# A streaming encoder layer: norm squares and block differences on VectorE, sample tokens at once, w_out summands a unit ahead, early sums first

## The chip, the core and the metric

The kernel runs on one core of a Trainium2 chip. The metric is the device time of one execution in microseconds; the time before is the median of three. In the rows PE is TensorE (PEld its weight loads), DVE is VectorE, ACT is ScalarE, POOL is GpSimd, and SP issues DMAs; ACTq and SPq are the DMA issues of ScalarE and SyncE.

## The reference

One layer is computed for 1024 prompt tokens and 32 sample tokens of width 1024:

```python
x = x + 0.5 * swiglu(rms_norm(x, ffn1_norm), ffn1_w_in, ffn1_w_out)   # hidden width 2816
h = rms_norm(x, mix_norm)
sq, sk, sv, hq, hf, hi, hg = split(h @ w_in)                          # 7 x 512 columns
sb_o = rms_norm(stick_breaking(rms_norm(sq), rms_norm(sk), sv))       # 8 heads of 64
o_h = rms_norm(hgrn2_scan(...)) * silu(hg)                            # 4 heads, 128 x 128
x = x + concat(sb_o, o_h) @ w_out
x = x + 0.5 * swiglu(rms_norm(x, ffn2_norm), ffn2_w_in, ffn2_w_out)
```

All is fp32. Besides the two x it returns the new keys, values and states.

## The kernel before

Everything is held transposed: 128 partitions are features, columns are tokens. A matrix product is three passes of fp32r matmuls, since each operand is split into a high part (a ScalarE copy, line 157) and a low part (a VectorE subtraction, line 158); `split` does both. The w_in product of each FFN, with its 2 x 2 blocks, and the second product are made of seven block products in place of eight, as in Strassen's scheme, so sums and differences of blocks are needed on both sides.

The stages follow one another: FFN1 (0 to about 735 us of the span), the mixers (to about 1440), the rest of w_out and FFN2. The order of instructions on each engine is written out when the program is built, from a planner's estimate of when each is ready and, among those ready, by the order of the source; inside `high_priority()` an instruction goes ahead of all others that are ready. On the chip each engine and each DMA queue then runs its list in order.

`prep_first` and `prep_rest` (from line 327) make the operands of an FFN's first product out of the four token-and-feature blocks b11, b12, b21, b22, once for each of two column parts of 256 and 272 columns. `prep_rest` takes four differences (line 336, the helper `sub`), each 1024 or 1088 columns wide; three run on VectorE and one, b22 - b12, on GpSimd. Line 316 scales a block by its norm.

`early_products` (line 343) runs the first two of the seven products for a few weight columns j (6 in FFN1, 8 in FFN2) before the operands of the others are there. ScalarE copies a product out of PSUM into a tile `e` (line 363), or VectorE adds one (line 365), and ScalarE's queue stores `e` to `pd` (line 367). In FFN2 from j = 2 the second product is accumulated in the same PSUM bank after the first was copied out. The tiles `e` are three buffers under the tag `xp`, which the mixers' small tiles and the w_out summands also use. `split_a` splits the weights of j + 2 (`wh`, `wl`), in two halves in FFN2 and whole in FFN1. The sums of the other weights (`rS`, lines 430 to 433) run on GpSimd for j = 0.

`Second.run` (from line 674) does an FFN's second product in 77 steps of 24 matmuls; line 643/644 split the weights (1024 columns), 654/655 the tokens `th`, `tl` (528 columns), 690 adds up blocks of x. In FFN1, `on1` calls `mix_in` in the last 22 steps and after each of the last four chunks, 16 times in all, for one chunk of 128 features and one half of the tokens. `mix_in` (line 1490) works on 512 prompt and then 16 sample columns: high part (1498), low part (1499), square (1501, 1504) and the sum of squares into `g.r` (1505, on GpSimd). `mix_factor` (1508) makes the norm's factor from `g.r`; that of half of the prompt tokens and of the sample tokens runs late, amid the mixers' first projections.

`mix_stream` (from line 1417) is the larger part of w_out: 8 chunks of 128 outputs in 3 token groups, 24 units of 18 matmuls. `g.slabs.get` loads weights (line 173, on SP). Each unit loads its summand `xp` from `xd` (line 1434, on SP), adds it to the product (1444, VectorE) and stores the sum (1445, on SP). `mix_units` (line 1459) follows with the rest of w_out.

Of the kernel before, what the change touches and what calls it, by code (L numbers as in the profile page):

```python
# [8 lines left out]
F32 = mybir.dt.float32  # L9
F32R = mybir.dt.float32r  # L10
U8 = mybir.dt.uint8
AF = mybir.ActivationFunctionType
ALU = mybir.AluOpType
AX = mybir.AxisListType
# [3 lines left out]
P = 128  # L18
D = 1024
KC = D // P  # L20
TP = 1024
TS = 32
T = TP + TS
GROUPS = ((0, 384), (384, 768), (768, T))
NG = len(GROUPS)
TG = 384
# [6 lines left out]
PASSES = ((0, 0), (0, 1), (1, 0))  # L33
# [113 lines left out]
def gs(n):  # L147
    return slice(*GROUPS[n])


def gw(n):
    return GROUPS[n][1] - GROUPS[n][0]


def split(nc, hi, lo, src):

    nc.scalar.activation(hi, src, AF.Copy)  # L157
    return nc.vector.tensor_tensor(out=lo, in0=src, in1=hi, op=ALU.subtract)  # L158
# [96 lines left out]
BW = 528  # L255
NB = 2
HK = KC // 2
# [70 lines left out]
def prep_rest(g, xc, rr, gain, xs, dst):  # L328

    nc = g.nc  # L330
    if xc is not None:
        for k in range(KC):
            scaled(nc.vector, dst[:, k, 1], xc[:, k, 1], gain, rr[:, 1], k)
    b11, b12 = dst[:, 0:HK, 0, :], dst[:, 0:HK, 1, :]
    b21, b22 = dst[:, HK:KC, 0, :], dst[:, HK:KC, 1, :]
    sub = lambda eng, out, p, q: eng.tensor_tensor(out=out, in0=p, in1=q, op=ALU.subtract)
    sub(nc.vector, b11, b12, b11)
    sub(nc.gpsimd, b12, b22, b12)
    split(nc, *xs["B22"], b22)
    sub(nc.vector, b22, b22, b11)  # L340
    sub(nc.vector, b21, b21, b22)
    for o, src in (("T2", b22), ("T1", b11), ("T3", b12), ("T4", b21)):
        split(nc, *xs[o], src)


def early_products(g, psp, xs, wts, pd, early, shared, between=None):

    nc = g.nc
    steps = [(p, j, c) for c in range(2) for j in range(2) for p in (1, 2)]
    for j in range(2, early):  # L350
        steps += [(1, j, 0), (1, j, 1), (2, j, 0), (2, j, 1)] if shared else [(p, j, c) for c in range(2) for p in (1, 2)]
    banks, tmps, done = {}, {}, 0
    for p, j, c in steps:
        w, cc = CW[c], cols(c)
        add = p == 2 and shared and j > 1
        wn, xn = PRODUCTS[p]
        if not add:
            banks[j, c] = psp.tile([P, 512], F32, name="bk", tag="bk", bufs=8)
        ps = banks[j, c][:, 0:w]
        products(g, ps, wts.get(j, wn), xs[c][xn], not add)  # L360
        tmp = g.wp.tile([P, CW[1]], F32, name=f"e{p}", tag="xp", bufs=3)[:, 0:w]
        if p == 1 or add:
            nc.scalar.activation(tmp, ps, AF.Copy)  # L363
        else:
            nc.vector.tensor_tensor(out=tmp, in0=ps, in1=tmps[j, c], op=ALU.add)
        tmps[j, c] = tmp
        nc.scalar.dma_start(pd[:, j, p - 1, cc], tmp)
        if p == 2:
            if c == 1 and j + 2 < early:
                wts.split_a(j + 2, 2 if shared else 1)  # L370
                if j + 4 < early:
                    wts.load_a(j + 4)
            if between is not None:
                between(done)
            done += 1
# [1043 lines left out]
def mix_stream(g, m, psp, xs, mix, xd):  # L1419

    nc = g.nc
    while not m.dup_done[3]:
        yield None
    for i, c in enumerate(MIX_FIRST):
        raw = m.sp.tile([P, T], F32, name="mraw", tag=("qn", "kn")[i % 2], bufs=1)
        nc.sync.dma_start(raw, mix[c])
        split(nc, xs(0, c), xs(1, c), raw)
    yield 5.0
    for d in range(KC):
        wt = g.slabs.get()  # L1430
        for n in range(NG):
            w = gw(n)
            xp = g.wp.tile([P, TG], F32, name="xp", tag="xp", bufs=3)
            nc.sync.dma_start(xp[:, 0:w], xd[:, d, gs(n)])
            ps = psp.tile([P, 512], F32, name="ps", tag="pp", bufs=2)
            for k, c in enumerate(MIX_FIRST):
                for i, (a, b) in enumerate(PASSES):
                    nc.tensor.matmul(ps[:, 0:w], wt[a][:, k, :], xs(b, c)[:, gs(n)],  # L1438
                                     start=(k == 0 and i == 0), stop=(k == 5 and i == len(PASSES) - 1))
                if n and k == 3:  # L1440
                    g.slabs.split_next()
                if k % 2:
                    yield 1.0
            nc.vector.tensor_tensor(out=xp[:, 0:w], in0=ps[:, 0:w], in1=xp[:, 0:w], op=ALU.add)
            nc.sync.dma_start(xd[:, d, gs(n)], xp[:, 0:w])
        m.spilled.append(d)
        m.fetch()

# [42 lines left out]
def mix_in(g, xs, pool, x, d, b):  # L1491

    nc = g.nc
    gain = g.gm[:, d:d + 1]
    for at, w, to in ((0, 512, 512 * b), (512, 16, TP + 16 * b)):
        src = x[:, d, b, at:at + w]
        hi, lo, acc = (t[:, to:to + w] for t in (xs(0, d), xs(1, d), g.r))
        nc.scalar.activation(hi, src, AF.Copy, scale=gain)
        nc.vector.scalar_tensor_tensor(out=lo, in0=src, scalar=gain, in1=hi, op0=ALU.mult, op1=ALU.subtract)
        if d == 0:  # L1500
            nc.scalar.activation(acc, src, AF.Square)
        else:
            sq = pool.tile([P, w], F32, name=f"nsq{w}", tag=f"nsq{w}", bufs=2)
            nc.scalar.activation(sq, src, AF.Square)  # L1504
            nc.gpsimd.tensor_tensor(out=acc, in0=acc, in1=sq, op=ALU.add)  # L1505


def mix_factor(g, ms, a, e):
# [14 lines left out]
def tile_layer(ctx: ExitStack, tc: tile.TileContext, *aps):  # L1523
# [132 lines left out]
    def on1(p, k):  # L1656
        if (p, k) == (6, FH - 1):
            qs.close()
            mx.stack, mx.pool = pool_of("xnp")
            mx.a = mx.pool.tile([P, 2, len(MIX_FIRST), T], F32R, name="xs_a", tag="xs_a", bufs=1)  # L1660
            mx.b = mx.pool.tile([P, 2, len(MIX_LAST), T], F32R, name="xs_b", tag="xs_b", bufs=1)
            tables(g, EXP_LN)
            todo.extend([(d, ROLE[0]) for d in range(HK)] + [(d, ROLE[1]) for d in range(HK)])
        elif (p, k) == (7, FH - 1):
            todo.extend((d, ROLE[1]) for d in range(HK, KC))
        elif p == "d":
            if k == 0:
                mix_factor(g, psp.tile([P, 512], F32, name="bk", tag="bk", bufs=8), 512 * ROLE[1], 512 * ROLE[1] + 512)
            mix_in(g, xs_mix, fbp, sec.x, HK + k, ROLE[0])
        elif todo and (p == 7 or p == 4 and k > 1):  # L1670
            with behind(g, sec.hi, sec.lo):
                mix_in(g, xs_mix, fbp, sec.x, *todo.pop(0))
        if (p, k) in ((4, FH - 3), ("d", 0)):
            g.slabs.ahead(1 if p == 4 else 2, whole=False)
        if (p, k) in ((4, FH - 2), ("d", 1)):
            for _ in range(2):
                g.slabs.split_next()
# [191 lines left out]
```

## Time and profile before

| | |
|---|---|
| median of 3 executions | 2187.49 us (2186.66 to 2188.24) |
| the profiled execution | 2183.27 us |
| its span, first to last instruction | 2181.5 us |
| granted TensorE clock, mean over the span | 0.995 of full speed |

The profile is of one execution, which took 4.22 us less than the median; 1.77 us of it lie outside its span. All stretches below are in microseconds from the span's start. A row of a timeline gives start, duration, engine, line, operation, the tile written and those read, the shapes, and in brackets the engine's idle time before it with what ended it. A waits row gives the waiter, what it waited for, microseconds in total, times, and the longest.

### The profile page before, as it was taken

Reading aid. Unit: us, or ns where it says so; the run is one execution under the profiler, and the core shown is the slowest. Engines: PE = TensorE matmul, PEld = TensorE weight load, DVE = VectorE, ACT = ScalarE, POOL = GpSimd, SP = SyncE. Lnnn points to the kernel's source line nnn. Section 1 sums busy time; section 2 is a strip of 40 time slices with the busy share of each in tenths; the row PEclk is TensorE's granted clock in tenths of the full one; section 3 lists DMA queues with packets and bytes.
Section 4 is the critical chain, followed back from the end, with each engine's and each line's share of the span. In section 5 each row is a group of like instructions: output and inputs, shape, how many; then the busy total and the mean of one; then the engine's idle time right before and its main releaser. Section 6 shows DMA issues by size and latency. Waiting matters only on the chain.

```text
span 2181.5 us, 41553 instructions
## 1 busy us (share of the span) xinstructions
PE 2123.6 (97%) x16331; PEld 2073.3 (95%) x16331; DVE 1476.6 (68%) x2537; ACT 937.5 (43%) x1836; POOL 631.9 (29%) x905
## 2 busy tenths in 40 slices
PE   8999999999999999999999999999999999999998
PEld 8999999999999899989899898889999999999998
DVE  5877666664678658778678688548677665655675
ACT  6423333333446555555564564235323332334443
POOL 1455544441002410311311311122555354420000
PEclk9999999999999999999999999999999999999999
DMA  8565454547534311120111212564775455466343
GB/s 242 177 215 171 149 175 147 160 145 262 211 117 158 104 55 29 44 70 21 54 59 29 69 58 88 169 199 139 224 225 179 160 163 163 155 212 241 123 149 124
DMA packets 328804, 307.28 MB, mean 141 GB/s; under 512 B 26592, under 2 KB 284896, under 8 KB 328608
## 3 DMA queue, kind: packets, MB, share of 16 engines
q1 hardware_dynamic: 259456, 264.75, 37.2%
q10 hardware_dynamic: 68672, 38.25, 6.0%
q8 instruction: 128, 2.10, 0.4%
q0 software_dynamic: 480, 1.62, 0.2%
q14 instruction: 68, 0.56, 0.1%
HBM read 208.46 MB, written 96.11 MB: 140 GB/s over the span
## 4 chain that ended last, share of the span: by engine, by line
PE 54%; DVE 4%; DMA 3%; POOL 2%; ACT 1%; issue 1%; SPq 0%; ACTq 0%; DVEq 0%; POOLq 0%
PE bk L382 17%; PE pp L833 14%; PE bk L697 10%; PE pl L1339 2%; PE av L1109 1%; PE ps L1438 1%; PE pt L1090 1%; DMA xd<-xp 1%; PE ps L1459 1%; PE z L1145 1%; PE z L1144 1%; DVE t L1003 1%; DMA oraw<-in_ffn_w_out_dram 1%; DMA xp<-xd 1%; PE pb L242 1%
## 5 line engine op out<-in xcount | busy, mean ns | idle before, releaser
L697 PE MATMUL bk<-tl,wh 128*128 128x256 f32 x1232 | 351.2, 285 | 4.6 <-DVE tl L655 4.5
L697 PE MATMUL bk<-th,wl 128*128 128x256 f32 x1232 | 350.0, 284 | 0.0
L697 PE MATMUL bk<-th,wh 128*128 128x256 f32 x1232 | 349.2, 285 | 0.5 <-ACT th L654 0.5
L833 PE MATMUL pp<-xs_a,wh 128*128 128x384 f32 (+1 forms) x1008 | 258.2, 338 | 0.0
L697 PEld LDWEIGHTS bk<-tl,wh 128*128 128x128 f32 x1232 | 232.5, 189 | 6.0 <-DVE tl L655 6.0
L697 PEld LDWEIGHTS bk<-th,wh 128*128 128x128 f32 x1232 | 231.7, 189 | 1.2 <-ACT th L654 0.9
L697 PEld LDWEIGHTS bk<-th,wl 128*128 128x128 f32 x1232 | 232.5, 189 | 0.2 <-issue 0.2
L833 PEld LDWEIGHTS pp<-xs_a,wh 128*128 128x128 f32 x1008 | 168.7, 189 | 5.9 <-issue 4.1
L644 DVE SCALAR_TENSOR_TENSOR wl<-oraw,wh 128x1024 fp32r<-128x1024 f32 x84 | 98.0, 1167 | 106.4 <-ACT wh L643 106.4
L537 POOL TENSOR_TENSOR gt<-gt,b 128x256 f32<-128x256 f32 x88 | 72.7, 826 | 325.1 <-ACT gt L536 325.1
L833 PE MATMUL pp<-xs_a,wl 128*128 128x384 f32 (+1 forms) x504 | 163.9, 325 | 0.0
L643 ACT ACTIVATE wh<-oraw 128x1024 fp32r<-128x1024 f32 x84 | 83.7, 996 | 147.4 <-PE bk L697 127.8
L382 PE MATMUL bk<-ops_a,wh 128*128 128x272 f32 (+1 forms) x704 | 132.9, 289 | 2.4 <-ACT e L363 2.4
L536 ACT ACTIVATE gt<-gt 128x256 f32<-128x256 f32 x88 | 37.3, 423 | 218.8 <-DVE gt L503 218.8
L157 ACT ACTIVATE wh<-wraw 128x512 fp32r<-128x512 f32 (+2 forms) x122 | 89.0, 749 | 93.4 <-PE pp L833 26.2
L158 DVE TENSOR_TENSOR wl<-wraw,wh 128x512 fp32r<-128x512 f32 (+2 forms) x122 | 107.7, 896 | 31.5 <-ACT wh L157 30.8
L382 PEld LDWEIGHTS bk<-ops_a,wh 128*128 128x128 f32 x704 | 111.2, 192 | 3.0 <-ACT e L363 2.9
L541 POOL TENSOR_TENSOR gt<-gt,b 128x256 f32<-128x256 f32 x88 | 90.1, 1024 | 78.2 <-DVE b L503 78.2
L382 PE MATMUL bk<-ops_a,wl 128*128 128x272 f32 (+1 forms) x352 | 101.1, 288 | 2.6 <-DVE wl L158 2.6
L503 DVE TENSOR_TENSOR gt<-bk,p 128x256 f32<-128x256 f32 (+1 forms) x60 | 25.9, 432 | 109.7 <-PE bk L382 107.8
L833 PEld LDWEIGHTS pp<-xs_a,wl 128*128 128x128 f32 x504 | 94.7, 188 | 0.1
L1505 POOL TENSOR_TENSOR rstd<-rstd,nsq 128x512 f32<-128x512 f32 (+1 forms) x28 | 33.4, 1218 | 205.1 <-ACT nsq L1504 205.1
(464 smaller groups left out, 6930.9 us busy)
## 6 DMA issues: line engine op xcount, KB each, us to landing
wraw<-in_ffn_w_in_dram SPq DMA_DIRECT2D x58, 512.0 KB, 4.3
oraw<-in_ffn_w_out_dram SPq DMA_DIRECT2D x94, 256.0 KB, 4.5
sd<-osum SPq DMA_DIRECT2D x44, 512.0 KB, 3.1
gd<-gt SPq DMA_DIRECT2D x42, 528.0 KB, 4.9
braw<-in_ffn_w_in_dram ACTq DMA_DIRECT2D x42, 512.0 KB, 4.3
oraw<-sd SPq DMA_DIRECT2D x40, 512.0 KB, 3.6
oraw<-in_ffn_w_out_dram SPq DMA_DIRECT2D x30, 512.0 KB, 3.3
wraw<-in_w_in_dram SPq DMA_DIRECT2D x28, 512.0 KB, 3.6
```

The lines of the kernel that those rows point to most:

```text
L157: nc.scalar.activation(hi, src, AF.Copy)
L158: return nc.vector.tensor_tensor(out=lo, in0=src, in1=hi, op=ALU.subtract)
L382: mm = g.nc.tensor.matmul(ps, wt[x][:, kk, :], xt[y][:, kk, :], start=(first and kk == 0 and n == 0), stop=(kk == HK - 1 and n == len(PASS ...
L536: silu = nc.scalar.activation(gt[:, 1, cc], gt[:, 1, cc], AF.Silu)
L537: nc.gpsimd.tensor_tensor(out=gt[:, 1, cc], in0=gt[:, 1, cc], in1=s["b2"], op=ALU.mult)
L541: last = nc.gpsimd.tensor_tensor(out=gt[:, 0, cc], in0=gt[:, 0, cc], in1=s["b1"], op=ALU.mult)
L643: nc.scalar.activation(h, r, AF.Copy, scale=0.5)
L644: nc.vector.scalar_tensor_tensor(out=l, in0=r, scalar=0.5, in1=h, op0=ALU.mult, op1=ALU.subtract)
L697: nc.tensor.matmul(ps, wt[a][:, d * P:(d + 1) * P], xt[b][:, cols(c)], start=(k == 0 and n == 0), stop=(k == FH - 1 and n == len(PASSES) - 1))
L833: g.filler = nc.tensor.matmul(ps[:, 0:gw(n)], wt[a][:, k, :], xs(b, k)[:, gs(n)], start=(k == 0 and j == 0), stop=(k == KC - 1 and j == le ...
L1339: nc.tensor.matmul(pl[0:L, c, 0:hl].rearrange("p (b m) -> p b m", m=m_), k[:, cs(b, c)], qr, start=True, stop=True)
L1505: nc.gpsimd.tensor_tensor(out=acc, in0=acc, in1=sq, op=ALU.add)
```

## The change

Five edits:

- The fourth difference of `prep_rest`, b22 - b12, moves from GpSimd to VectorE, for both column parts of both FFNs.
- In `early_products` the copies and adds out of PSUM get high priority, and so do the splits of the weights of j + 2, which are now in two halves in FFN1 too.
- In `mix_stream` the load of a unit's summand is issued a unit ahead, that of the first unit before the loop.
- `mix_in` leaves out the sample columns, and its sum of squares moves from GpSimd to VectorE.
- A new function, `mix_in_sample`, does the sample columns of all eight chunks at once, after the last `mix_in` of the second product: one square, one reduction, one multiplication by the gain, and three splits.

```diff
-    sub(nc.gpsimd, b12, b22, b12)
+    sub(nc.vector, b12, b22, b12)
...
-            if p == 1 or add:
-                nc.scalar.activation(tmp, ps, AF.Copy)
-            else:
-                nc.vector.tensor_tensor(out=tmp, in0=ps, in1=tmps[j, c], op=ALU.add)
+        with g.tc.high_priority():
+            if p == 1 or add:
+                nc.scalar.activation(tmp, ps, AF.Copy)
+            else:
+                nc.vector.tensor_tensor(out=tmp, in0=ps, in1=tmps[j, c], op=ALU.add)
...
-                wts.split_a(j + 2, 2 if shared else 1)
+                with g.tc.high_priority():
+                    wts.split_a(j + 2, 2)
...
+    units = [(d, n) for d in range(KC) for n in range(NG)]
+    def summand(d, n):
+        xp = g.wp.tile([P, TG], F32, name="xp", tag="xp", bufs=3)
+        nc.sync.dma_start(xp[:, 0:gw(n)], xd[:, d, gs(n)])
+        return xp
+    nxt = summand(*units[0])
...
+    for u, (d, n) in enumerate(units):
+        if n == 0:
+            wt = g.slabs.get()
+        w, xp = gw(n), nxt
+        if u + 1 < len(units):
+            nxt = summand(*units[u + 1])
...
-    for at, w, to in ((0, 512, 512 * b), (512, 16, TP + 16 * b)):
...
-            nc.gpsimd.tensor_tensor(out=acc, in0=acc, in1=sq, op=ALU.add)
+        nc.vector.tensor_tensor(out=acc, in0=acc, in1=sq, op=ALU.add)
+def mix_in_sample(g, mx, pool, x):
+    src = x[:, :, :, 512:BW]
+    t = pool.tile([P, KC, NB, 16], F32, name="smx", tag="nsq", bufs=2)
+    nc.scalar.activation(t, src, AF.Square)
+    nc.vector.tensor_reduce(out=g.r[:, TP:T].rearrange("p (b s) -> p b s", b=NB),
+                            in_=t.rearrange("p k b s -> p b s k"), axis=AX.X, op=ALU.add)
+    t = pool.tile([P, KC, NB * 16], F32, name="smx", tag="nsq", bufs=2)
+    nc.vector.tensor_tensor(out=t.rearrange("p k (b s) -> p k b s", b=NB), in0=src,
+                            in1=g.gm[:, :, None, None].broadcast_to([P, KC, NB, 16]), op=ALU.mult)
+    for dst, ks in ((mx.a[:, :, 0:3, TP:T], slice(0, 3)), (mx.b[:, :, :, TP:T], slice(3, 8, 4)),
+                    (mx.a[:, :, 3:6, TP:T], slice(4, 7))):
+        split(nc, dst[:, 0], dst[:, 1], t[:, ks])
...
             mix_in(g, xs_mix, fbp, sec.x, HK + k, ROLE[0])
+            if k == HK - 1:
+                mix_in_sample(g, mx, fbp, sec.x)
```

## Rows read from the trace of the kernel before

**Rows 1.** The page's part 1: busy us, share of the span, instructions.
```profile
PE 2123.6 (97%) x16331; PEld 2073.3 (95%) x16331; DVE 1476.6 (68%) x2537; ACT 937.5 (43%) x1836; POOL 631.9 (29%) x905
```

**Rows 2.** Waits of TensorE, whole span: total us, times, longest us.
```profile
PE bk L697 <- DVE tl L655: 4.5, 4, 2.5
...
PE bk L382 <- DVE wl L158: 3.5, 2, 2.6
...
PE bk L382 <- ACT e L363: 2.4, 2, 1.7
PE ps L1459 <- DVE xp L1444: 2.1, 1, 2.1
...
PE bk L382 <- ACT S2h L157: 1.4, 1, 1.4
...
PE ps L1438 <- DVE xp L1444: 0.9, 1, 0.9
```

**Rows 3.** Windows: stretch, length, busy (count) PE PEld DVE ACT POOL, clock, DMA.
```profile
682.16:685.57 3.41, 3.19 (x14) 3.19 (x15) 3.41 (x6) 1.06 (x4) 1.93 (x2) 0.50 0.72 232
1494.53:1497.94 3.41, 3.41 (x18) 3.41 (x17) 3.41 (x6) 1.94 (x4) 0.00 (x0) 0.50 0.79 240
560.00:563.41 3.41, 3.41 (x30) 3.41 (x29) 1.31 (x2) 1.17 (x2) 0.00 (x0) 1.00 0.83 321
```

**Rows 4.** Timeline of VectorE, 1486 to 1494 us, FFN2's early products.
```profile
1485.57 0.48 DVE L316 SCALAR_TENSOR_TENSOR x<-x,g,rr 128x256 f32<-128x256 f32 x1
...
1488.57 2.64 DVE L316 SCALAR_TENSOR_TENSOR x<-x,g,rr 128x272 f32<-128x272 f32 x1
...
1491.48 1.21 DVE L336 TENSOR_TENSOR x<-x 128x1024 f32<-128x1024 f32 x1
1492.61 1.28 DVE L158 TENSOR_TENSOR wl<-wraw,wh 128x512 fp32r<-128x512 f32 x2
```

**Rows 5.** Timeline of GpSimd in the same stretch: the difference that moves.
```profile
1487.59 3.31 POOL L336 TENSOR_TENSOR x<-x 128x1024 f32<-128x1024 f32 x1 [11.95 <-DVE x L336]
```

**Rows 6.** Timeline of VectorE, 669 to 684 us, mix_in amid FFN1's second product.
```profile
670.17 0.89 DVE L1499 SCALAR_TENSOR_TENSOR xs_a<-x,gm,xs_a 128x512 fp32r<-128x512 f32 x2
...
673.28 0.70 DVE L655 TENSOR_TENSOR tl<-rw,th 128x528 fp32r<-128x528 f32 x1
673.90 1.94 DVE L1499 SCALAR_TENSOR_TENSOR xs_a<-x,gm,xs_a 128x512 fp32r<-128x512 f32 x2
...
679.39 2.30 DVE L644 SCALAR_TENSOR_TENSOR wl<-oraw,wh 128x1024 fp32r<-128x1024 f32 x1
```

**Rows 7.** Timeline of GpSimd, 660 to 750 us: the sums that move.
```profile
673.21 8.56 POOL L1505 TENSOR_TENSOR rstd<-rstd,nsq 128x512 f32<-128x512 f32 x6 [166.49 <-ACT nsq L1504]
```

**Rows 8.** Windows, columns as in rows 3: from the first mix_in steps to TensorE's wait.
```profile
664.90:682.38 17.48, 14.42 (x114) 13.78 (x112) 17.48 (x19) 17.45 (x40) 8.56 (x6) 0.99 0.56 187
```

**Rows 9.** Timeline of VectorE, 745 to 748 us: the last mix_in.
```profile
745.60 0.91 DVE L1499 SCALAR_TENSOR_TENSOR xs_b<-x,gm,xs_b 128x512 fp32r<-128x512 f32 x2
```

**Rows 10.** Timeline of TensorE, 754 to 757 us: first reader of the sample columns' sums.
```profile
754.01 1.17 PE L1510 MATMUL nms<-rstd,ones 128*128 128x512 f32 x4
```

**Rows 11.** Timeline of ScalarE, 1524 to 1531 us, end of FFN2's early products.
```profile
1528.61 1.10 ACT L157 ACTIVATE T41h<-x 128x1088 fp32r<-128x1088 f32 x1
...
1529.61 0.37 ACT L363 ACTIVATE e<-bk 128x256 f32<-128x256 f32 x1
```

**Rows 12.** Timeline of SP's queue, 1398 to 1412 us, w_out.
```profile
1404.93 0.33 SPq L1445 DMA_DIRECT2D xd<-xp  x1
1405.55 0.33 SPq L1434 DMA_DIRECT2D xp<-xd  x1
```

**Rows 13.** The summand loads, line 1434: count, first and last start, time to landing.
```profile
L1434 SPq DMA_DIRECT2D xp<-xd x24: 319/324/530, 1323.4 to 1439.2; - x24
...
DMA to landing us min/median/max: 2.1/2.8/5.8
```

**Rows 14.** The stores of the sums, line 1445: time to landing.
```profile
DMA to landing us min/median/max: 1.7/2.6/6.0
```

More of the change, by code (lines that the diff above doesn't have):

```diff
@@ L1427, in mix_stream @@
         split(nc, xs(0, c), xs(1, c), raw)
-    yield 5.0
[L1429 to L1445, printed above, removed]
+    units = [(d, n) for d in range(KC) for n in range(NG)]
[4 more added lines that the diff above has]
+    nxt = summand(*units[0])
+    yield 5.0
+    for u, (d, n) in enumerate(units):
[4 more added lines that the diff above has]
+            nxt = summand(*units[u + 1])
+        ps = psp.tile([P, 512], F32, name="ps", tag="pp", bufs=2)
+        for k, c in enumerate(MIX_FIRST):
+            for i, (a, b) in enumerate(PASSES):
+                nc.tensor.matmul(ps[:, 0:w], wt[a][:, k, :], xs(b, c)[:, gs(n)],
+                                 start=(k == 0 and i == 0), stop=(k == 5 and i == len(PASSES) - 1))
+            if n and k == 3:
+                g.slabs.split_next()
+            if k % 2:
+                yield 1.0
+        nc.vector.tensor_tensor(out=xp[:, 0:w], in0=ps[:, 0:w], in1=xp[:, 0:w], op=ALU.add)
+        nc.sync.dma_start(xd[:, d, gs(n)], xp[:, 0:w])
+        if n < NG - 1:
+            continue
         m.spilled.append(d)
@@ L1494, in mix_in @@
     gain = g.gm[:, d:d + 1]
-    for at, w, to in ((0, 512, 512 * b), (512, 16, TP + 16 * b)):
[L1496 to L1504, printed above, removed]
-            nc.gpsimd.tensor_tensor(out=acc, in0=acc, in1=sq, op=ALU.add)
+    at = slice(512 * b, 512 * b + 512)
+    src = x[:, d, b, 0:512]
+    hi, lo, acc = (t[:, at] for t in (xs(0, d), xs(1, d), g.r))
+    nc.scalar.activation(hi, src, AF.Copy, scale=gain)
+    nc.vector.scalar_tensor_tensor(out=lo, in0=src, scalar=gain, in1=hi, op0=ALU.mult, op1=ALU.subtract)
+    if d == 0:
+        nc.scalar.activation(acc, src, AF.Square)
+    else:
+        sq = pool.tile([P, 512], F32, name="nsq", tag="nsq", bufs=2)
+        nc.scalar.activation(sq, src, AF.Square)
+        nc.vector.tensor_tensor(out=acc, in0=acc, in1=sq, op=ALU.add)
+def mix_in_sample(g, mx, pool, x):
+    nc = g.nc
+    src = x[:, :, :, 512:BW]
[9 more added lines that the diff above has]
+        split(nc, dst[:, 0], dst[:, 1], t[:, ks])
 def mix_factor(g, ms, a, e):
```

## Prediction

> **What bounds the kernel now.** The page first: TensorE is busy for 2123.6 of 2181.5 us [rows 1]. The change adds and removes no matmul, so at most those 57.9 idle us are to be had, and what a lowered clock costs. So TensorE's waits come next. Of the groups that the five edits can touch, the reader sees six: on the low part of the second product's tokens `tl` 4.5 us (longest 2.5), on the early weights `wl` 3.5 (2.6), on the early tiles `e` 2.4, on the w_out sums `xp` 2.1 and 0.9, and on the first weight sums S2 1.4 [rows 2]. Then the windows: two stretches of 3.41 us around the two longest of these were granted 0.50 of the clock, which is its 1.2 GHz level, against 1.00 (2.4 GHz) elsewhere. They hold 14 and 18 matmuls, where 3.41 us at the full level hold 30 [rows 3]. TensorE had just stood still for 2.5 and 2.6 us. One matmul takes 3.41/30 = 0.114 us, so the drop costs 12 x 0.114 = 1.4 us in the second stretch; in the first, with 3.19 us of busy time, 28 would have fitted, so 14 x 0.114 = 1.6. I count 1.5 for a drop. Last, VectorE and GpSimd at the two longest waits, part by part below.
>
> **The difference b22 - b12.** On GpSimd it ran from 1487.59 to 1490.90 us [rows 5]. On VectorE a scaling of 272 columns began at 1488.57 and took 2.64 us, ending 0.3 us behind GpSimd; its sibling of 256 columns took 0.48 [rows 4]. So 2.16 us of VectorE were lost while GpSimd ran. Behind the stretched instruction stood the next `e` sum, the difference at 1491.48 (1.21) and then the two halves of `wl` at 1492.61 [rows 4], for which TensorE waited 2.6 us [rows 2]. After the change VectorE makes the difference itself, at 1.21 as its like of 1024 columns. The loss of 2.16 goes, and the 1.21 comes in. If the halves of `wl`, now of high priority, go ahead of both differences, they are 2.16 + 1.21 = 3.4 us early and the wait of 2.6 is gone, with its clock drop. If they stay behind both, they are 2.16 - 1.21 = 0.95 early. I take the first, 2.6 + 1.5 = 4.1 us; ends 0.95 and 4.1. The other three differences stand where rows 2 shows no wait of this size; VectorE's idle time covers them (32% of the span, [rows 1]), and without that cover they cost up to 3 x 1.21 = 3.6.
>
> **The sums of squares.** From 664.90 to 682.38 us VectorE was busy without a gap, and ScalarE for 17.45 of 17.48 [rows 8]; at the end TensorE waits 2.5 for `tl`. A pair of low parts took 0.89 us when GpSimd stood still and 1.94 with its sums alongside [rows 6, 7]; one more such pair lies in the stretch. The weights' low part at 679.39 took 2.30, where 1024 columns alone take about 1.21 [rows 4, 6]. On VectorE a sum over 512 columns should take what 528 do, 0.70 [rows 6]. So in this stretch: the first pair loses its 16 columns (0.89 to 0.70, a gain of 0.19), two pairs become 0.70 + 0.70 in place of 1.94 (0.54 each), and the weights' split gets 1.09 back: 0.19 + 1.08 + 1.09 = 2.36. ScalarE loses two short instructions per call, so it isn't late in VectorE's place. The wait shrinks from 2.5 to about 0.15, the smaller waits on `tl` there go with it, and the clock drop ends: 2.36 + 1.5 = 3.9. Ends: with both waits there (2.9) gone 4.4; if VectorE won nothing back from GpSimd, three sums of 0.70 on a full engine would lose 2.1.
>
> The Trainium skill speaks against this part: its Perfetto Trace Analysis, section Optimizing Scalar/DVE Operations, says that where VectorE is saturated, moving work to ScalarE or even GpSimd may make sense, and adds that the two share a read port, so it may not help. By the first half the sum would hold the loss of 2.1 where I count a gain of 3.9, and the time would be 6.0 us more. The stretched rows here agree with its second half.
>
> **The sample columns at once.** Per call two instructions on ScalarE, one on VectorE and one on GpSimd go, 16 times; nine come, once, four on ScalarE and five on VectorE, none with more than 256 columns, so at most 0.48 each [rows 4]: 2.4 us on VectorE. They come after the last low parts, which end at 746.5 [rows 9], and so end by about 749; the first reader of their sums starts at 754.01 [rows 10]. That cover of 5 us makes them free. They stand on VectorE ahead of the first projections' reductions, which without a gap would cost up to 1.
>
> **Weights in halves.** In FFN1 the other wait on `wl` is 3.5 - 2.6 = 0.9 us [rows 2]. TensorE needs the first half first, and that is ready one half's time, 0.64 [rows 4], earlier on VectorE and about as much on ScalarE, so the wait goes. But what is late next is S2 (1.4 us, [rows 2]), whose sums wait for stored tiles to come back and not for TensorE: arriving 0.9 sooner, it waits 0.9 longer. I take 0; ends 0.9 lost and 0.9 won.
>
> **Early sums first.** At the end of FFN2's early products ScalarE made an operand for 1.10 us at 1528.61 and the copy `e` after it, at 1529.61 [rows 11]; TensorE waited for that copy. With priority it goes ahead of the operand: 1.0 us. The waits for `e` come to 2.4 [rows 2]; the rest stands behind weight sums of GpSimd, which this edit doesn't move. Ends 0 and 2.4; I take 1.0.
>
> **The summands.** A load at 1405.55 stood on SP behind a store at 1404.93 that needed VectorE's sum [rows 12]. A unit earlier in the source, it goes ahead of that store, and ahead of the next weights' two loads where a new chunk begins; the add that TensorE waited 0.9 for then has its summand. The later wait, 2.1 with a drop, I leave in the sum: only three buffers carry loads and stores, and a load can't start before an older store has landed, however early it is asked for. Ends 0 and 0.9 + 2.1 + 1.5 = 4.5; I take 0.9.
>
> **The sum.** 4.1 + 3.9 + 0 + 0 + 1.0 + 0.9 = 9.9 us. The profiled execution took 2183.27, so 2173.4; it lies 4.2 below the median of 2187.49, which by the same sum goes to 2177.6 (ratio 0.9955).
>
> **Rivals.** About 0.2%, 4.4 us, is what a measurement of this kernel can tell from no change, so the borders of no change are 2183.1 and 2191.9.
>
> Everything goes (4.1, 4.4, 0.9, 2.4, 4.5, together 16.3): 2171.2. For it speak the many short waits with one cause; against, that orders are planned anew and some waits come back.
>
> The waits come back: the halves of `wl` stay behind both differences (0.95, clock drop kept) and the moved sums stand ahead of `tl` (two of 0.70 off 2.36 leave 0.95); nothing else: 1.9 won, 2185.6, no change. For it speaks that VectorE is full in both places [rows 4, 8].
>
> The moved sums only load VectorE: nothing comes back from GpSimd, and three sums of 0.70 on a full engine lose 2.1 where 3.9 were counted, so 9.9 - 6.0 = 3.9 are won, 2183.6. For it speaks the full engine [rows 8], against it the stretched pairs [rows 6]. It is what the first half of the sentence of the Trainium skill's Perfetto Trace Analysis, Optimizing Scalar/DVE Operations, comes to here.
>
> Slower, by the summands' buffers. From 1323.4 to 1439.2 the 24 loads start 115.8/23 = 5.0 us apart [rows 13], so each of three buffers may be held for 15.0. It is held for the load (median 2.8), VectorE's sum (0.5) and the store (2.6, [rows 14]), 5.9; asked for a unit ahead, for 5.0 more: 10.9, and nothing is lost. With the longest landings, 5.8 and 6.0, it is 17.3, so 5.8 a unit, 0.8 x 24 = 19 us lost, against 9.0 from the other edits: 2197.5. It decides from 15.0 on, where load and store together take 9.5 us rather than 5.4.
>
> **How the numbers follow.** Chances: forecast 0.53, everything goes 0.13, waits come back 0.18, moved sums only load VectorE 0.06, slower 0.10. The forecast's own range, with its terms' ends, is 2173 to 2182. The range 2169 to 2188 takes in all but the slower rival and some 0.05 beyond its ends. Faster 0.66, the first two; same 0.24, the next two; slower 0.10.
>
> **What would show it.** Right: no difference on GpSimd, and no VectorE scaling over 0.6 us in the early products; low parts of 512 columns at 0.70 throughout; TensorE's waits on `wl` near 0 and on `tl` under 2.5 in all; two clock drops fewer. Wrong: the granted clock still 0.50 in FFN1's last steps or FFN2's early products, a longer wait on S2, ScalarE held up for an `xp` buffer, or new waits in the mixers, whose order is planned anew.

## The result, and the profile after

The changed kernel takes 2173.66 us, the kernel before beside it 2186.64 (medians of 8 executions each): ratio 0.9946, 95% interval 0.9933 to 0.9959. Measured again later it was 0.9958 (0.9945 to 0.9972). The forecast, 2177.6 from 2187.49, is a ratio of 0.9955. The profiled execution's span is 2172.3 us, after 2181.5. In the changed kernel line numbers are one or two higher in FFN1's and FFN2's code (L382 is L384) and ten to twelve higher in w_out and `mix_in`.

The page's part 1, as in [rows 1]; GpSimd lost 46 us of work and VectorE, which took it over, 7:

```profile
PE 2118.7 (98%) x16331; PEld 2069.1 (95%) x16331; DVE 1469.8 (68%) x2548; ACT 933.2 (43%) x1812; POOL 585.6 (27%) x873
```

TensorE's waits, as in [rows 2]:

```profile
PE bk L384 <- DVE S4l L158: 7.3, 5, 2.9
PE bk L752 <- issue: 3.4, 1, 3.4
...
PE ps L1448 <- ACT wh L157: 2.0, 1, 2.0
PE ms L1499 <- POOL rr L1481: 1.6, 1, 1.6
PE ps L1471 <- DVE xp L1454: 1.5, 1, 1.5
...
PE bk L384 <- ACT e L364: 1.1, 2, 0.8
...
PE bk L699 <- DVE tl L657: 0.8, 2, 0.6
```

Two groups of the kernel before that [rows 2] leaves out:

```profile
PE bk L382 <- DVE S4l L158: 4.1, 5, 1.5
...
PE bk L750 <- issue: 1.9, 1, 1.9
```

The reader sees what went: the early products' wait on `wl`, 3.5 us, is gone from the list, `tl` is down from 4.5 to 0.8, `e` from 2.4 to 1.1. And what came: in FFN1 the wait for the last rows' transposes (L752, "issue") was 1.9 and is 3.4. The waits on the weight sums S4 were 4.1 over the whole span and are 7.3: 2.8 and 4.3 of it in FFN1, 1.3 and 2.9 in FFN2. In w_out there is a wait on `wh`, in its end one on `rr`. The windows, as in [rows 3]: the two drops shown of before are gone, and two stand in FFN1, behind the two longer waits (besides the one at the end there are five in the whole trace before, two here). The third row stands behind a wait of 2.5 us in w_out's rest; here the clock stays up.

```profile
46.87:50.28 3.41, 3.41 (x19) 3.41 (x18) 1.95 (x3) 2.42 (x3) 1.27 (x1) 0.50 1.18 292
101.48:104.89 3.41, 3.41 (x16) 3.41 (x16) 3.14 (x7) 0.00 (x0) 1.66 (x2) 0.50 0.88 288
1464.65:1468.06 3.41, 2.44 (x18) 2.23 (x18) 3.30 (x8) 2.70 (x8) 2.25 (x3) 1.00 0.41 141
```

VectorE's timeline in FFN2's early products, which answers to [rows 4]: five scalings take 2.06 together where one of 272 columns took 2.64, the difference is an ordinary 1.21, and the two halves of `wl` run at 1.28 in the middle of the operands. GpSimd is idle from 1470 to 1494 us.

```profile
1477.69 2.06 DVE L316 SCALAR_TENSOR_TENSOR x<-x,g,rr 128x256 f32<-128x256 f32 x5
...
1480.01 1.21 DVE L336 TENSOR_TENSOR x<-x 128x1024 f32<-128x1024 f32 x1
...
1482.28 1.21 DVE L336 TENSOR_TENSOR x<-x 128x1024 f32<-128x1024 f32 x1
...
1483.76 1.28 DVE L158 TENSOR_TENSOR wl<-wraw,wh 128x512 fp32r<-128x512 f32 x2
1484.96 1.22 DVE L336 TENSOR_TENSOR x<-x 128x1024 f32<-128x1024 f32 x1
```

The order is neither of the two that the forecast weighed. The halves of `wl` stand behind the moved difference (1482.28) and ahead of the next one alone (1484.96), and the scaling of 272 columns has left this place for a later one. From the first difference to `wl` it is 3.75 us (1480.01 to 1483.76); in the kernel before it was 6.31, from the row below to 1492.61 in [rows 4]. So `wl` comes 2.56 us sooner.

```profile
1486.30 1.21 DVE L336 TENSOR_TENSOR x<-x 128x1024 f32<-128x1024 f32 x1
```

The same amid FFN1's second product, which answers to [rows 6]: the weights' split takes 1.22 (2.30 before), one low part 0.74 (a pair took 1.94), the new sum of squares 0.68.

```profile
673.12 1.22 DVE L646 SCALAR_TENSOR_TENSOR wl<-oraw,wh 128x1024 fp32r<-128x1024 f32 x1
...
674.88 0.74 DVE L1511 SCALAR_TENSOR_TENSOR xs_a<-x,gm,xs_a 128x512 fp32r<-128x512 f32 x1
675.54 0.68 DVE L1517 TENSOR_TENSOR rstd<-rstd,nsq 128x512 f32<-128x512 f32 x1
```

Where FFN1 lost time is on VectorE's timeline before 47 us, first of the changed kernel, then of the kernel before:

```profile
39.22 0.44 DVE L366 TENSOR_TENSOR e<-bk,e 128x272 f32<-128x272 f32 x1 [1.97 <-DMA pd<-e]
...
40.78 0.28 DVE L740 TENSOR_SCALAR dg<-ident,r 128x128 f32<-128x128 f32 x1
...
46.16 0.29 DVE L740 TENSOR_SCALAR dg<-ident,r 128x128 f32<-128x128 f32 x1 [1.51 <-POOL r L738]
```

```profile
44.58 0.29 DVE L738 TENSOR_SCALAR dg<-ident,r 128x128 f32<-128x128 f32 x1 [0.80 <-POOL r L736]
```

A sum `e`, now ahead of all that is ready, stood 1.97 us idle until the store of an older `e` gave its buffer free. Behind it in VectorE's order waited the norm's transposed tokens, which VectorE takes out of PSUM, and the diagonal `dg` (40.78, 39.29 before). The delay then passes through ScalarE's square of the last rows (44.08, 42.49 before) and GpSimd's factor `r` (45.30, 43.72 before) to the last `dg` (46.16, 44.58 before), for which TensorE waits. How long the hold is varies: in the second profile of the changed kernel the same sum stood 0.90 us, the last `dg` began at 44.60, and TensorE still waited 2.8. What the priority costs here is therefore read from the experiments below.

### The profile page after: what moved, and what is told of

It reads as the page before. It is cut to its first block, busy times and chain, and to the rows that moved or that the text cites. A ratio compares the mean times of both kernels' runs of the same rounds, so it can differ in the third digit from the quotient of the medians.

```text
span 2172.3 us, 41486 instructions
## 1 busy us (share of the span) xinstructions
PE 2118.7 (98%) x16331; PEld 2069.1 (95%) x16331; DVE 1469.8 (68%) x2548; ACT 933.2 (43%) x1812; POOL 585.6 (27%) x873
## 4 chain that ended last, share of the span: by engine, by line
PE 53%; DMA 5%; DVE 4%; POOL 1%; ACT 1%; issue 1%; SPq 0%; DVEq 0%; ACTq 0%; POOLq 0%
PE bk L384 16%; PE pp L835 14%; PE bk L699 10%; PE pl L1341 2%; PE ps L1448 2%; PE av L1111 1%; PE pt L1092 1%; DMA xd<-xp 1%; PE ps L1471 1%; PE z L1147 1%; PE z L1146 1%; DMA wraw<-in_ffn_w_in_dram 1%; DMA braw<-in_ffn_w_in_dram 1%; DVE t L1005 1%; DMA oraw<-in_ffn_w_out_dram 1%
## 5 line engine op out<-in xcount | busy, mean ns | idle before, releaser
L384 PE MATMUL bk<-ops_a,wh 128*128 128x272 f32 (+1 forms) x704 | 131.8, 287 | 1.3 <-ACT e L364 1.1
L384 PEld LDWEIGHTS bk<-ops_a,wh 128*128 128x128 f32 x704 | 110.0, 190 | 2.2 <-ACT e L364 2.2
L384 PE MATMUL bk<-ops_a,wl 128*128 128x272 f32 (+1 forms) x352 | 100.5, 286 | 0.1
L1003 ACT ACTIVATE t<-z,minus 128x128 f32<-128x128 f32 (+2 forms) x96 | 55.4, 577 | 67.8 <-PE z L1149 48.8
```

The lines of the kernel that those rows point to most:

```text
L384: mm = g.nc.tensor.matmul(ps, wt[x][:, kk, :], xt[y][:, kk, :], start=(first and kk == 0 and n == 0), stop=(kk == HK - 1 and n == len(PASS ...
L1003: nc.scalar.activation(a, z, AF.Sigmoid, scale=minus)
```

## The experiments

Twelve more runs were made. To tell stages apart I take the start of given matmuls in each trace, since every kernel has the same number of them on each line: stage I ends at the 155th matmul of FFN1's second product, Ia (its first part) at the 309th of the block products; II (second product and `mix_in`) at the first projection; III is w_out, from its first matmul to the last of `mix_units`; IV goes from there to the 617th block matmul of FFN2, past the early products. The stretch between II and III took 582.2 to 583.9 us in all kernels, and that behind IV 605.0 to 607.7; there the kernel before has the least of all, and the other thirteen have 606.4 on average.

```
kernel                              median us  ratio (95%)               Ia     I      II     III    IV
before                              2186.64    1                         75.8   524.4  214.0  155.2  85.5
changed                             2173.66    0.9946 (0.9933, 0.9959)   77.8   525.3  208.9  153.2  80.8
changed, again                      2176.20    0.9958 (0.9945, 0.9972)   76.3   522.5  209.1  154.1  80.9
difference back on GpSimd           2179.99    0.9964 (0.9950, 0.9977)   78.6   528.0  209.5  154.7  84.4
sums back on GpSimd                 2182.57    0.9978 (0.9967, 0.9989)   78.7   525.4  214.8  151.8  81.7
no priority, FFN1 weights whole     2175.63    0.9948 (0.9935, 0.9960)   75.6   523.5  209.2  151.8  82.5
summands not ahead                  2179.03    0.9963 (0.9951, 0.9976)   75.9   524.5  209.7  158.0  81.4
sample columns call by call         2176.11    0.9952 (0.9939, 0.9964)   77.5   526.0  210.6  157.1  81.0
additions added on GpSimd           2183.44    0.9978 (0.9970, 0.9987)   77.4   524.8  215.6  155.0  81.5
copies added on GpSimd              2178.24    0.9961 (0.9947, 0.9974)   78.7   526.2  211.3  154.7  80.6
priority in FFN2 alone              2172.93    0.9932 (0.9920, 0.9945)   75.6   521.8  210.4  154.4  80.5
  and weights first in FFN1         2181.94    0.9983 (0.9974, 0.9992)   75.7   529.8  208.9  154.5  81.3
  and chunks fetched later          2172.86    0.9940 (0.9927, 0.9952)   75.3   524.5  209.3  153.3  80.8
  and summands not ahead            2175.94    0.9956 (0.9943, 0.9970)   75.3   521.7  209.7  155.8  80.8
```

A ratio is to the kernel before on the same chip; medians of different rows need not be. The stage columns, in us, are of one profiled execution each. Where an edit doesn't touch a stage they show what an execution adds of its own: about 1.5 us in II, 1.2 in IV, but 5 in III and in I, where much waits for DMAs.

**The difference back on GpSimd.**

```diff
-    sub(nc.vector, b12, b22, b12)
+    sub(nc.gpsimd, b12, b22, b12)
```

> The changed kernel (2173.7 us) with only the difference b22 - b12 back on GpSimd, in both FFNs. The prediction's theory: in FFN2's early products VectorE's scaling of 272 columns is stretched from about 0.5 to 2.6 us again while GpSimd runs, the halves of wl come later, TensorE waits some 2.6 us for them and the granted clock falls to 0.50 for 3.4 us: 4.1 us slower, 2177.8, all of it lost between 1480 and 1540 us of the span. Rival 1, the priority of wl alone had cured the wait: under 0.5 us lost, 2173.9, no wait on wl above 0.5. Rival 2, only what VectorE gets back net counts (0.95): 2174.6.

Stage IV took 84.4 us; the eleven kernels that have the difference on VectorE and the priority in FFN2 took 80.5 to 81.7, mean 81.0. So 3.4 us. GpSimd's timeline, VectorE's, TensorE's waits and the window of this kernel:

```profile
1486.44 3.31 POOL L336 TENSOR_TENSOR x<-x 128x1024 f32<-128x1024 f32 x1 [11.75 <-DVE x L336]
```

```profile
1487.41 2.65 DVE L316 SCALAR_TENSOR_TENSOR x<-x,g,rr 128x272 f32<-128x272 f32 x1
```

```profile
PE bk L384 <- DVE wl L158: 2.6, 1, 2.6
```

```profile
1492.08:1495.50 3.42, 3.31 (x15) 3.31 (x16) 3.42 (x7) 1.97 (x4) 0.00 (x0) 0.50 0.55 166
```

All four signs of before are back, though `wl` has its priority. Rival 1 falls, and so does rival 2 with its 0.95.

**The sums back on GpSimd.**

```diff
-        nc.vector.tensor_tensor(out=acc, in0=acc, in1=sq, op=ALU.add)
+        nc.gpsimd.tensor_tensor(out=acc, in0=acc, in1=sq, op=ALU.add)
```

> The changed kernel with only mix_in's sums of squares back on GpSimd (the sample columns stay at once). The prediction's theory: pairs of low parts at 1.9 us in place of 1.4 and a stretched weight split beside the 8.6 us of GpSimd's sums, the wait of 2.5 us on tl back, with its clock drop: 3.9 us slower, 2177.6, all of it between 660 and 700 us. Rival, the sums only load VectorE and the gain of the stage comes from the sample columns: three sums of 0.70 us come off a full VectorE, 2.1 us faster, 2171.6; TensorE doesn't wait for tl.

Stage II took 214.8 us. The nine kernels without GpSimd work in it and with the sample columns at once took 208.9 to 210.4, mean 209.4: 5.4 us, more than the 3.9. VectorE, GpSimd, TensorE's waits:

```profile
684.44 1.80 DVE L1511 SCALAR_TENSOR_TENSOR xs_a<-x,gm,xs_a 128x512 fp32r<-128x512 f32 x1
...
687.34 2.31 DVE L646 SCALAR_TENSOR_TENSOR wl<-oraw,wh 128x1024 fp32r<-128x1024 f32 x1
```

```profile
684.41 1.29 POOL L1517 TENSOR_TENSOR rstd<-rstd,nsq 128x512 f32<-128x512 f32 x1 [4.04 <-ACT nsq L1516]
687.16 1.41 POOL L1517 TENSOR_TENSOR rstd<-rstd,nsq 128x512 f32<-128x512 f32 x1 [1.46 <-ACT nsq L1516]
```

```profile
PE bk L699 <- DVE tl L657: 5.2, 6, 2.1
```

Beside one sum on GpSimd the low part takes 1.80 in place of 0.74, beside the next the split 2.31 in place of 1.22: each costs VectorE 1.06 to 1.09 us, and VectorE's own sum costs it 0.68. So the full engine gains 0.4 us by taking a sum over. The rival, that the sums only load VectorE, is refuted in sign.

**Work on GpSimd that no one reads.** Two kernels add to the changed kernel, behind each sum of squares, additions or copies into a scratch tile:

```diff
+        for h in range(2):
+            z = pool.tile([P, 256], F32, name="gz", tag="gz", bufs=1)
+            nc.gpsimd.tensor_tensor(out=z, in0=src[:, 256 * h:256 * h + 256], in1=src[:, 256 * h:256 * h + 256], op=ALU.add)
```

> The changed kernel with work added that no one reads: in each mix_in that sums squares, GpSimd also adds the chunk to itself, twice 256 columns, into a scratch tile. VectorE's and ScalarE's instructions are unchanged. If GpSimd's two-input additions stretch VectorE's instructions beside them, as the prediction read it: low parts and weight splits of up to 2.3 us between 670 and 695 us, the waits on tl back at 2 us or more with a clock drop, 4 to 8 us slower: 2177.7 to 2181.7. Rival, the stage was late because the sums themselves came late on GpSimd: no change, 2173.7.

> As the kernel with added additions on GpSimd, but each of the added instructions is a copy with one input in place of an addition with two. If any work of GpSimd on the same memory stretches VectorE: as there, 4 us slower or more, 2177.7 and up. If only two-input work does: low parts of 512 columns stay at 0.75 us and the time at 2173.7, within 0.5 us by 700 us of the span.

Stage II became 215.6 with the additions (6.2 more than the mean of 209.4) and 211.3 with the copies (1.9). VectorE's and ScalarE's instructions are those of the changed kernel, in the same order, and no one waits for the scratch tile; so the time comes from GpSimd's running alone. With the additions, GpSimd, VectorE, TensorE's waits:

```profile
668.96 8.28 POOL L1520 TENSOR_TENSOR gz<-x 128x256 f32<-128x256 f32 x6 [25.68 <-DVE x L692]
```

```profile
672.53 1.10 DVE L1511 SCALAR_TENSOR_TENSOR xs_a<-x,gm,xs_a 128x512 fp32r<-128x512 f32 x1
...
675.14 1.63 DVE L646 SCALAR_TENSOR_TENSOR wl<-oraw,wh 128x1024 fp32r<-128x1024 f32 x1
676.69 1.11 DVE L657 TENSOR_TENSOR tl<-rw,th 128x528 fp32r<-128x528 f32 x1
```

```profile
PE bk L699 <- DVE tl L657: 6.1, 5, 2.7
```

With the copies, VectorE:

```profile
673.82 0.88 DVE L1511 SCALAR_TENSOR_TENSOR xs_a<-x,gm,xs_a 128x512 fp32r<-128x512 f32 x1
...
675.99 1.41 DVE L646 SCALAR_TENSOR_TENSOR wl<-oraw,wh 128x1024 fp32r<-128x1024 f32 x1
```

Each VectorE instruction beside an addition of 256 columns takes 0.36 to 0.41 us longer here, whatever its own length (0.74 to 1.10, 1.22 to 1.63, 0.70 to 1.11), beside a copy 0.14 to 0.20 (0.74 to 0.88, 1.22 to 1.41, 0.70 to 0.90). The expectation that copies cost either nothing or as much as additions was wrong on both sides: they cost about half as much for each instruction.

**Sample columns call by call.** `mix_in` as before with both widths, its sums on VectorE, without `mix_in_sample`:

```diff
-    at = slice(512 * b, 512 * b + 512)
...
+    for at, w, to in ((0, 512, 512 * b), (512, 16, TP + 16 * b)):
...
-            if k == HK - 1:
-                mix_in_sample(g, mx, fbp, sec.x)
```

> The changed kernel with mix_in's 512 and then 16 columns call by call as before, sums of squares on VectorE, mix_in_sample left out. The prediction's theory (the sample columns at once are worth 0): 2173.7, at most 0.5 us lost by 700 us of the span. Rival, they hold a part of the 5.8 us that the sums' return to GpSimd cost: two more VectorE instructions and two more of ScalarE per call in the stretch where both are full; six calls with 0.2 us for each instruction, 2.4 on VectorE: up to 2.4 slower, 2176.1, and waits on tl of 1 us and more by 700 us.

Stage II took 210.6, 1.2 above the mean and 0.2 above the longest of the nine: 0 to 1.2 us, so the forecast's 0 holds to about 1 us. The 157.1 us of stage III are w_out's, which this edit leaves alone.

**Without priority; with priority in FFN2 alone.** The first takes `high_priority()` off the sums `e` and off the weights, which FFN1 splits whole again. The second keeps both for FFN2:

```diff
-        with g.tc.high_priority():
+        with g.tc.high_priority() if shared else nullcontext():
             if p == 1 or add:
...
-                with g.tc.high_priority():
-                    wts.split_a(j + 2, 2)
+                with g.tc.high_priority() if shared else nullcontext():
+                    wts.split_a(j + 2, 2 if shared else 1)
```

> The changed kernel without the high priority in the early products, of the sums e and of the weights, which are split whole in FFN1 as before. Theory now, from the trace after: in FFN1 a sum e with priority held VectorE for 2.0 us until its buffer's store had ended, the last diagonal came 1.6 us later and TensorE waited 3.4 instead of 1.9 us at 45 us, with a clock drop: without priority the first 60 us give back 3.1 us, of which 1 to 2 are lost again at S2 and S4 by 160 us; FFN2 loses 1.0 on e. Net 0 to 1 us faster, 2172.7 to 2173.7. The prediction's theory (0 in FFN1, 1.0 won in FFN2): 1.0 us slower, 2174.7, and FFN1's start as late as with priority. Rival, the priority of wl is what cured FFN2's wait of 2.6 us: 3 us slower or more, 2176.7.

> The changed kernel (2173.7 us) with the high priority in FFN2's early products alone; in FFN1 the sums e and the weights, whole, as before. Theory: FFN1's start isn't held any more by a sum e that waits for its buffer's store (TensorE's wait at 45 us back from 3.4 to 1.9, no clock drop there: 3.1 us by 50 us of the span), S2 and S4 take 1 to 2 of it back by 160 us; FFN2 keeps its 1.0. So 1 to 2 us faster than the changed kernel, 2171.7 to 2172.7. Rival, what comes early in FFN1 waits in full for the stored tiles of S2 and S4: 2173.7, with 3 us more of waits on S2 and S4.

Without any, stage IV took 82.5, 1.5 above the mean of 81.0: that is what the priority, of the sums `e` and of the weights together, is worth in FFN2. Of the wait of 2.6 us on `wl` only one of 0.4 stands there, later (1511 us), so it was the difference that cured it. By its ratio, 0.9948, the kernel is even with the changed one: what FFN2 loses without priority, FFN1 wins back. Ia takes 75.3 to 75.8 in the five kernels without priority in FFN1, mean 75.5, and 75.9 to 78.7 in the eight with the changed kernel's, mean 77.6: 2.1 us lost, and stage I as a whole differs by as much (523.2 and 525.3). TensorE's wait is back at that of before, 1.9 us in both kernels; in the second:

```profile
PE bk L753 <- ACT B220h L158: 1.9, 1, 1.9
```

With priority in FFN2 alone, ratio 0.9932, the kernel has the lowest ratio of all; both ratios of the changed kernel lie above its, though the intervals overlap. FFN1's start did what the theory said; the whole gain, 3.1 and 5.7 us by the two ratios, is more than the 1 to 2 expected, and its size isn't settled.

**And weights first in FFN1.** As the last kernel, but FFN1's weights in halves with priority:

```diff
-                with g.tc.high_priority() if shared else nullcontext():
-                    wts.split_a(j + 2, 2 if shared else 1)
+                with g.tc.high_priority():
+                    wts.split_a(j + 2, 2)
```

> The changed kernel with the sums e of high priority in FFN2 alone, and the weights in halves of high priority in both FFNs. Theory: in FFN1 it is the sum e that holds VectorE for its buffer, not the weights: TensorE's wait at 45 us is 1.9 and FFN1's start 2.7 us earlier, as with no priority in FFN1 at all; 2171.7 to 2173.7. Rival, the halves of the weights delay the last diagonal: wait of 3.2 to 3.4 as in the changed kernel, 2173.7.

Half right: Ia is 75.7, so it is the sum `e` that holds FFN1's start. But the next 308 matmuls took 51.7 us where the others took 42.0 to 44.7, and the time is the worst of all. TensorE's waits and VectorE's timeline:

```profile
PE bk L385 <- DVE S4l L159: 7.5, 3, 5.1
```

```profile
119.82 0.42 DVE L506 TENSOR_TENSOR u<-bk,p 128x256 f32<-128x256 f32 x1 [5.69 <-DMA p<-pd]
120.16 0.68 DVE L159 TENSOR_TENSOR S4l<-rS,S4h 128x512 fp32r<-128x512 f32 x1
```

S4's low part stands on VectorE behind a sum that waits 5.69 us for a stored product to come back; with priority in FFN2 alone the same sum, at 111.84 us, waited 2.90. The products come earlier, but what they meet doesn't. Why the stored product comes as late as this isn't shown.

**Summands not ahead, twice**, once in the changed kernel and once with priority in FFN2 alone:

```diff
-    nxt = summand(*units[0])
...
-        w, xp = gw(n), nxt
-        if u + 1 < len(units):
-            nxt = summand(*units[u + 1])
+        w, xp = gw(n), summand(d, n)
```

> The changed kernel with the load of a summand back at the start of its own unit. The trace after has lost 2.0 us against before at 1420 us (a wait of 2.0 on wh) and won 3.4 by 1474 us, where a clock drop is gone. Theory: the loads a unit ahead made both; without them the wait of 0.85 us on xp is back and the wait of 2.0 on wh gone, then the drop back: 1 to 2 us slower, 2174.7 to 2175.7. Rival, the drop's end has nothing to do with the loads, but with the time at which the stage begins: 0 to 2 us faster, 2171.7 to 2173.7. Against the expectation of a hold on the three buffers: no wait for a buffer of xp in either.

> The kernel with priority in FFN2 alone (ratio 0.9932), with the load of a summand back at the start of its own unit: a second sample of what the loads a unit ahead are worth, which the prediction put at 0.9 us and the first removal at 3.7 by medians. If 0.9 is right and the rest was the execution's own: ratio under 0.994, VectorE's sums wait for their summands as often, but TensorE no more than 1 us longer in w_out. If 3.7 is right: ratio 0.9945 to 0.996 (2176 to 2179 us), TensorE waits 3 us and more for a sum of VectorE at 1440, and the granted clock falls to 0.50 in w_out's last units.

What VectorE's sums (line L1451 here) waited for without the loads ahead, and the same of the changed kernel (L1454): us and times.

```profile
  DMA xp<-xd: 20.0, 8
  PE ps L1445: 4.9, 5
```

```profile
  PE ps L1448: 14.9, 10
  DMA xd<-xp: 3.7, 1
  DMA xp<-xd: 2.8, 1
```

VectorE now waits for TensorE, as it should, and less for DMAs: 20.0 came down to 3.7 + 2.8 = 6.5 in the changed kernel, and in the second pair 15.9 to 6.5 (before: 12.7). For TensorE this is worth less. Stage III without the loads ahead took 155.2, 158.0 and 155.8, with them 151.8 to 157.1, mean 154.1 of ten: 2.2 us, inside what executions differ by. By medians it is 0.0011 of 2187 (from the mean of the two ratios of the changed kernel) and 0.0024, 2.4 and 5.2 us. So more than 0.9 is likely, and its size stays open. In the second kernel the expected wait of 3 us didn't come (it was 2.0), though the ratio did.

**The changed kernel again, and chunks fetched later.** The second has priority in FFN2 alone and asks for a finished chunk's loads into FFN2's input one chunk later:

```diff
-        m.spilled.append(d)
         m.fetch()
+        m.spilled.append(d)
```

> The changed kernel itself, once more, beside the two that follow: 2173.7 us. Its profile tells what an execution adds of its own: in kernels with the same lines there, TensorE's last wait for a summand's sum at 1440 us is 1.0 to 1.5 us in some and 3.2 to 3.7 in others. If that varies between executions of one program, it stands anywhere between 0.9 and 3.7 here; if the program sets it, it is 1.5 within 0.3.

> The kernel with priority in FFN2 alone (2172.9), and in w_out the loads of finished chunks into FFN2's input are asked for one chunk later, so that ScalarE's queue doesn't stand at a load that waits for a store just issued. Theory: ScalarE's idle time of 8.7 us before 1419 us goes, the wait of 2.0 to 2.6 us on wh at 1419 goes with it, and what is late next is the summand's sum at 1440 (1.0 to 3.7): 1 to 2 us faster, 2171 to 2172. Rival, the loads of the last chunks now come so late that the adds of w_out's rest wait for them: 2173 to 2175, with waits of 2 us and more between 1440 and 1465.

In the second profile of the changed kernel the last wait for a summand's sum is 0.4 us, and was 1.5: it belongs to the execution, and a single profile can't price it. With the later loads the wait on `wh` (2.0 and 2.7 in the changed kernel, 2.6 with priority in FFN2 alone) is gone and one of 1.3 on a sum stands near it; stage III took 153.3, nothing gained that could be told.

## Why the prediction was right

**The bound.** The gain came out of TensorE's waits and its clock. The ratio forecast, 0.9955, lies between the two measured, and by the stages the terms stand thus, before against the means above:

- Difference and early sums, stage IV: 85.5 - 81.0 = 4.5, forecast 4.1 + 1.0 = 5.1. Singly, by removal, 3.4 and 1.5. The first was taken at its upper end, and the wait and the drop did both go. The step to it didn't hold: `wl` didn't go ahead of both differences, 3.4 us early, but of one, and not by its priority, since without priority `wl` stands in the same place. It came 2.56 sooner, by the stretch and by a scaling that the new order puts elsewhere. That this is just about the wait of 2.6 is luck. The second term was a little short.
- Sums of squares and sample columns, stage II: 214.0 - 209.4 = 4.6, by removal of the sums alone 5.4, forecast 3.9 + 0. The mechanism was that of the forecast, low parts 0.74 for 0.70 and splits 1.22 for 1.21. In this stage the waits on `tl` went from 2.9 to 0.2 (rows below), which with the drop of 1.5 is 4.2, and the forecast's upper end was 4.4 by the same count. The rest of the 4.5 before, 0.56 and 0.97, stands at 504 and 523 us, ahead of the first `mix_in`: 1.5 is there again in the second profile of the changed kernel, whose `tl` is 1.8 in all, so the 0.8 of the first owes a part to its execution. With the sums back on GpSimd the stage's waits on `tl` are 3.7, more than before; why isn't shown.
- Summands, stage III: 155.2 - 154.1 = 1.1, by removal 2.2, forecast 0.9; not settled.
- Weights in halves and `e` in FFN1, stage I: 524.4 - 525.3 = -0.9, forecast 0, at the end of its range. Here a step failed: "early sums first" was priced in FFN2 alone. In FFN1 the same edit costs 2.1 us, which the kernel with weights first puts down to the sum `e`, and the trace to its wait for a buffer. The forecast had named a hold on an `xp` buffer among the signs of error, but on ScalarE; it was VectorE. "What is late next is S2" was right in kind, but it was S4: in FFN1 S2's waits went from 2.7 to 1.4 and S4's from 2.8 to 4.3.

The waits on `tl` between 660 and 720 us, before and after:

```profile
PE bk L697 <- DVE tl L655: 2.9, 2, 2.5
```

```profile
PE bk L699 <- DVE tl L657: 0.2, 1, 0.2
```

Together 4.5 + 4.6 + 1.1 - 0.9 = 9.3 us, forecast 9.9. That the totals meet is in part luck. The gain in the sums of squares was larger than forecast and makes up for most of what FFN1 lost; behind stage IV the kernel before has 1.5 us less than the others, which takes the 9.3 to 7.8; and by the medians 13.0 us were won, measured again 10.7, since the kernel before was profiled in an execution shorter than its median (2183.27, 2186.64). The signs named came true: no difference on GpSimd, no long scaling, no `wl` wait in the early products, `tl` at 0.8 and 1.8, the two drops gone. Two new ones in FFN1 had not been foreseen (in the second profile one there, and two more in w_out and its rest).

**The rivals.** "The waits come back" had the wait on `wl` kept with its drop and most of that on `tl`; both are gone. "The moved sums only load VectorE" is refuted by the sums' return, which costs VectorE more than the same sums done on VectorE, and by the added additions, which alone bring the waits back. The rival was the first half of what the Trainium skill's Perfetto Trace Analysis, section Optimizing Scalar/DVE Operations, says; its warning in the second half, that moving work between VectorE and GpSimd might not help, is what holds here. "Slower, by the summands' buffers" didn't come: with the loads ahead VectorE waited less for DMAs, not more. The hold itself is there: in the changed kernel four loads in a row start within 0.1 us of an older store's landing (at 1410.08, 1415.25, 1419.15 and 1422.32; landed at 1410.06, 1415.18, 1419.09 and 1422.31). But TensorE's waits for the sums are 1.5 us in all, and 0.4 in the second profile. "Everything goes" was too much: S4, FFN1's start, `wh` and `rr` took their places.

## What to carry to other kernels

Before counting moved work as load on a full VectorE, look at what VectorE's instructions take while the other engine runs: here a 512-column sum cost VectorE 1.06 to 1.09 us from GpSimd, where GpSimd was first, and 0.68 done by itself. Priority for an instruction that may wait (for a buffer's store, for a load) holds all that stands behind it on its engine: give it only where its buffers are free, as in FFN2 and not in FFN1. And products that come earlier won nothing here where their next operands waited for DMAs.

## What was not expected of the hardware

Where GpSimd is first, VectorE pays. In the rows above, a VectorE instruction with both inputs in SBUF, the cores' on-chip memory, loses beside one GpSimd instruction 0.14 to 0.20 us for a copy of 256 columns, 0.36 to 0.41 for an addition of 256 (of a tile to itself), 1.06 to 1.09 for a sum of 512, and 2.65 - 0.48 = 2.17 for a difference of 1024; it doesn't depend on VectorE's own length. GpSimd's row isn't the price, since it can hold GpSimd's own waiting too, as the rows below show: the additions that cost 0.4 are 8.28/6 = 1.38 us long.

It isn't a fixed price either. In FFN1's block products of the kernel before, a low part that begins 0.04 us behind a GpSimd sum takes 1.28 us; one that begins 0.04 us ahead of the same sum takes 0.69, and there GpSimd's row is 1.29 in place of 0.78:

```profile
193.64 1.28 DVE L158 TENSOR_TENSOR A22l<-braw,A22h 128x512 fp32r<-128x512 f32 x1
...
213.81 0.69 DVE L158 TENSOR_TENSOR A22l<-braw,A22h 128x512 fp32r<-128x512 f32 x1
```

```profile
193.60 0.78 POOL L541 TENSOR_TENSOR gt<-gt,b 128x272 f32<-128x272 f32 x1
...
213.85 1.29 POOL L541 TENSOR_TENSOR gt<-gt,b 128x272 f32<-128x272 f32 x1 [0.23 <-DVE b L503]
```

And a VectorE sum with one input in PSUM lost nothing: `u<-bk,p` takes 0.41 to 0.45 us in all 88 cases, also where it lies wholly beside a GpSimd sum:

```profile
187.60 0.43 DVE L503 TENSOR_TENSOR u<-bk,p 128x272 f32<-128x272 f32 x1
```

```profile
186.55 1.74 POOL L480 TENSOR_TENSOR osum<-oraw 128x256 f32<-128x256 f32 x1
```

The Trainium skill's SBUF — State Buffer, section SBUF: two separate sides, says that the two share a pair of ports as an exclusive lock, held for a whole instruction by the one that starts first, while the other is blocked, and that of VectorE's ordinary instructions those with two SBUF inputs take part. These rows agree.

The clock isn't a matter of the wait's length alone. Behind the wait of 2.5 us in w_out's rest, the same in both profiles of the changed kernel, it stayed at 1.00 in the first (shown above) and fell to 0.50, its 1.2 GHz level, in the second:

```profile
1462.67:1466.08 3.41, 3.41 (x15) 3.41 (x16) 2.90 (x6) 2.43 (x6) 2.27 (x3) 0.50 0.42 143
```

All fourteen profiles have this wait, of 2.47 to 2.51 us. In five of them the clock stood at 0.50 from within 1.0 us of its end, in nine it stayed at 1.00.

So a drop that stands in one profile, some 1.5 us, is counted on with less right than the wait ahead of it.
